# Modulation pieces of the later sections: loaded one step ahead of their sums, at other rates, and cut into two streams

## The chip, the cores and the metric

One core of a Trainium2 chip runs the whole program. The metric is device time in microseconds (us) of one execution. TensorE does the matmuls, VectorE (DVE) and ScalarE (ACT) the elementwise work, GpSimd (POOL) a little, SyncE (SP) issues nearly all loads. The time before is 2664.92 us, the median of 3 runs.

## The reference, cut to what matters

The program computes two transformer-like blocks on 256 tokens of width 2048. All that the change touches lies in the first block:

```python
mod = (c_act @ w_mod + b_mod)[:, None, :]          # w_mod: 2048 x 12288
sh1, sc1, gt1, sh2, sc2, gt2 = jnp.split(mod, 6, axis=-1)
h = rmsnorm(x, g_norm1) * (1 + sc1) + sh1
...                                                # projections w_in, GLA and mLSTM scans
x = x + gt1 * merge_groups(...)                    # ends in a product with w_out
h2 = rmsnorm(x, g_norm2) * (1 + sc2) + sh2
x = x + gt2 * conv_ffn(h2, ...)                    # w_up, a 3x3 convolution, w_down
```

The modulation vector `mod` is one vector of 2048 times a matrix of 2048 x 12288. Its six sections of 2048 columns are wanted at different times: sections 0 and 1 at once, section 2 (`gt1`) in the product with `w_out`, sections 3 and 4 (`sh2`, `sc2`) at the norm ahead of the FFN, section 5 (`gt2`) at the end of the FFN.

## The kernel before, in words

**Weights.** Every large product reads its weight in units of 512 KB (128 partitions x 1024 floats). `units` (from L189) yields them; `load_raw` (L168 to L173) takes one of the four `raw` buffers and has SP load it (L172). `split_w` then makes two halves of the number: ACT casts `raw` into `wh` (L187), DVE subtracts into `wl` (L188). There are four `wh` and four `wl` buffers. When L188 is done the `raw` buffer is free. TensorE multiplies from `wh` and `wl`: `a_form` has three matmuls per tile (L208 to L210), `b2_form` two (L237, L238).

**Modulation beside the weights.** Sections 2 to 5 are summed on DVE, not on TensorE. They make 16 blocks of 512 columns, and `mod_vec` treats a block in 8 steps. A step loads 512 KB of `w_mod` through the same `load_raw` and the same four `raw` buffers, and adds two rows of it, each scaled, into the tile `ev` (L514 for the first row of a block, L516 for the others). After the eighth step a small matmul (L523, L533 or L543) adds over the partitions and the result goes into `gtd` (section 2), `mod` (3 and 4) or `gtr` (5).

**What sets the order.** `Stream.tick` is called once per weight unit and takes `rate` steps of the stream. `MODS` holds the rates by part of the program: the second half of the inputs, keys (8 units of the mLSTM keys, and then 8 units of the GLA queries, for which no other rate is set), values (16 units), gates (40 units), output (32 units of `w_out`), FFN (240 units). A second stream, `side`, issues the scans' work in the same way. Up to the values SP follows the order of the code; from the gates on the framework's scheduler orders SP too. On the other engines it orders by readiness and by place in the code, with a bonus for L187 and L188. Each engine works through its own queue in order: an instruction that waits holds up what stands behind it.

**The end of `mix_out`.** After the last unit of `w_out` a loop (L1197) takes steps until twelve blocks are done, because the norm needs sections 3 and 4. Then `ple_fill(4)` gives TensorE four small products of the second block, `norm_T` makes `h2`, and the FFN begins. `x` is updated at L1189 and L1190, the row scale is made from L1214 and L258, the normalised rows are scaled at L1233 and L314. The second block has a place of the same shape, the product with `pool_w_out` (64 units, `out_product`) and what follows it, without any modulation beside it.

Of the kernel before, what the change touches and what calls it, by code (L numbers as in the profile page):

```python
# [6 lines left out]
F32 = mybir.dt.float32  # L7
# [3 lines left out]
ALU = mybir.AluOpType  # L11
# [3 lines left out]
P = 128  # L15
D = 2048
# [8 lines left out]
OUTG = ((0, 512), (512, 512), (1024, 512), (1536, 256), (1792, 256))  # L25
NG = len(OUTG)

MODS = {"inputs": 1.0, "keys": 1.0, "values": 1.25, "gates": 0.75, "output": 0.5, "ffn": 0.15}

SIDE = {"keys": 1.0, "queries": 1.0, "values": 1.4, "gates": 1.6, "attention": 1.3}  # L30
AHEAD = 1000
# [75 lines left out]
class Kern:  # L107
# [391 lines left out]
                nc.vector.tensor_tensor(out=dst, in0=dst, in1=wide(self.g1 if sec == 1 else self.g2), op=ALU.mult)  # L499
        yield 1  # L500

    def mod_vec(self, sec, blk):


        nc, a = self.nc, self.a
        c0 = sec * D + blk * 512
        ev = self.one([P, 512], "ev")
        for k0 in range(0, 16, 2):
            src = a["w_mod"][0, k0 * P:(k0 + 2) * P, c0:c0 + 512].rearrange("(k p) n -> p k n", p=P)
            _, rv = self.load_raw(src, 2, 512)  # L510
            for i in range(2):
                cc = self.cs[:, 2 * (k0 + i):2 * (k0 + i) + 1]
                if k0 + i == 0:
                    nc.vector.tensor_scalar(out=ev, in0=rv[:, i, :], scalar1=cc, scalar2=None, op0=ALU.mult)  # L514
                else:
                    nc.vector.scalar_tensor_tensor(out=ev, in0=rv[:, i, :], scalar=cc, in1=ev,  # L516
                                                   op0=ALU.mult, op1=ALU.add)
            if k0 < 14:
                yield 1
        if sec == 2:  # L520

            pt = self.ps()
            nc.tensor.matmul(pt[0:1], self.c("one"), ev, start=True, stop=True)  # L523
            b, g = self.t2(), self.t2()
            nc.sync.dma_start(b[0:1], a["b_mod"][0:1, c0:c0 + 512])
            nc.vector.tensor_tensor(out=g[0:1], in0=pt[0:1], in1=b[0:1], op=ALU.add)
            nc.scalar.dma_start(self.gtd[:, blk * 512:(blk + 1) * 512], g[0:1])
            yield 1
            return
        if sec == 5:  # L530

            pt = self.ps()
            nc.tensor.matmul(pt, self.c("one").broadcast_to([P, P]), ev, start=True, stop=True)  # L533
            if blk % 2 == 0:
                self.gtr.append(self.t4())
            b = self.t2()
            nc.sync.dma_start(b, a["b_mod"][0, c0:c0 + 512].partition_broadcast(P))
            nc.vector.tensor_tensor(out=self.gtr[-1][:, (blk % 2) * 512:(blk % 2 + 1) * 512], in0=pt, in1=b, op=ALU.add)
            yield 1
            return  # L540
        pv = self.ps()[:, :8].rearrange("p (k r) -> p k r", r=2)
        for q in range(4):
            nc.tensor.matmul(pv[:, q, :], ev[:, q * P:(q + 1) * P], self.c("one").broadcast_to([P, 2]),  # L543
                             start=True, stop=True)
        s = slice(blk * 4, blk * 4 + 4)
        wide = lambda v: v[:, s].unsqueeze(2).broadcast_to([P, 4, 2])
        dst = self.mod[sec][:, s, :]
        nc.vector.tensor_tensor(out=dst, in0=pv, in1=wide(self.bm[sec]), op=ALU.add)
        if sec == 4:
            nc.vector.tensor_tensor(out=dst, in0=dst, in1=wide(self.g2), op=ALU.mult)  # L550
        yield 1

    def mod_steps(self):
        self.gtr = []
        self.gtd = self.dram.tile([1, D], F32, name="gtd")
        for b in range(16):
            yield from self.mod_vec(2 + b // 4, b % 4)
            self.mods_done = b + 1


    def mix_in(self):
        nc, a = self.nc, self.a
# [25 lines left out]
        gates = self.t2((112, 2, T))  # L588
# [4 lines left out]
        blocks = [(k, k + 2) for k in range(0, 16, 2)]  # L593
        nb = len(blocks)

        def mod_block(b):
            lo, hi = blocks[b]
            return self.mod_pe(lo * P, (hi - lo) * P, (0, 1))

        def hidden(b, ti):  # L600
            kts = list(range(*blocks[b]))
            x, dst = (self.xt[2:4], hl) if ti == 0 else (self.xt[0:2], hc)
            self.xposed([(lambda kt, tt=tt: x[kt // 8][:, tt, kt % 8 * P:(kt % 8 + 1) * P]) for tt in range(2)], kts, dst,
                        scale=lambda kt: self.a1[:, kt, ti:ti + 1], shift=lambda kt: self.s1[:, kt, ti:ti + 1])
# [31 lines left out]
        def weights(b, i):  # L636
            if b < nb:
                ws[b, i] = list(self.units(w, 512 + 512 * i, 512, range(*blocks[b])))
# [10 lines left out]
        for b in range(nb):  # L649
            mods = mod_block(b + 1) if b + 1 < nb else iter(())  # L650

            if b == nb // 2:
                self.setup_later()
                self.mods_done = 0
                self.mods.set(self.mod_steps(), MODS["inputs"])
            weights(b + 1, 0)
            for i, _ in enumerate(pieces(b)):
                if i == 4:
                    weights(b + 1, 1)
                if i == 8:  # L660
                    weights(b + 1, 2)
                if i % 2 == 0:
                    next(mods, None)
                if i == 8 and b + 1 < nb:
                    hidden(b + 1, 0)
                if i == 10 and b + 1 < nb:
                    hidden(b + 1, 1)
# [25 lines left out]

        self.mods.rate = MODS["keys"]
        self.side.set(self.gla_context(gkc, gvc), SIDE["keys"])
# [10 lines left out]
        self.queries = True  # L706
        self.mods.rate = MODS["values"]
        self.side.rate = SIDE["values"]
# [200 lines left out]
    def mix_scan(self):  # L909
        nc, a = self.nc, self.a  # L910
        w = a["w_in"][0]
        self.mods.rate = MODS["gates"]
        gm = self.b8((P, 3, T))
# [248 lines left out]
    def mix_out(self):  # L1162
        nc, a = self.nc, self.a
        self.side.drain()
        self.mods.rate = MODS["output"]
        self.x = []
        for tt in range(2):
            t = self.b8()
            nc.sync.dma_start(t, a["x"][0, tt * P:(tt + 1) * P, :])
            self.x.append(t)  # L1170
        yT = self.act_pair(16)

        def src(tt):
            def f(kt):
                y = self.ygla if kt < 8 else self.yml
                return y[:, tt, (kt % 8) * P:(kt % 8 + 1) * P]
            return f
        self.xposed([src(0), src(1)], list(range(16)), yT)
        sums = self.sums(1)
        for g, (c0, n) in enumerate(OUTG):  # L1180
            s = slice(c0, c0 + n)
            gt = self.t2()[:, :n]
            nc.sync.dma_start(gt, self.gtd[0, s].partition_broadcast(P))
            accs = self.a_group(a["w_out"][0], c0, yT, range(16), n)
            with self.urgent(g == NG - 1):
                for tt in range(2):
                    t = self.t2()[:, :n]
                    x = self.x[tt][:, s]
                    nc.vector.tensor_tensor(out=t, in0=accs[tt], in1=gt, op=ALU.mult)  # L1189
                    nc.vector.tensor_tensor(out=x, in0=t, in1=x, op=ALU.add)  # L1190
                    self.square_sum(x, sums[:, 0, tt, g:g + 1])
        self.tap("x1", self.x[0])

        self.x1 = self.dram.tile([2, P, D], F32, name="x1")
        for tt in range(2):
            nc.sync.dma_start(self.x1[tt], self.x[tt])
        while self.mods_done < 12:  # L1197
            self.mods.step()
        self.ple_fill(4)
        with self.urgent():  # L1200
            rs = self.rstd(self.total(sums, 1)[:, 0], D, 2)
            self.h2 = self.norm_T(self.x, rs, scale=lambda kt: self.a2[:, kt, 0:1],
                                  shift=lambda kt: self.s2[:, kt, 0:1])
        self.mods.rate = MODS["ffn"]
        self.five = True

    def sums(self, kinds):
# [647 lines left out]
```

## Time and profile before

| what | value |
|---|---|
| median of 3 runs | 2664.92 us (2662.52 to 2669.27) |
| the profiled execution: its time / span of its instructions | 2672.57 us / 2670.4 us |
| share of the span: TensorE matmul, weight load, DVE, ACT | 97%, 82%, 69%, 48% |
| moved by the DMA engines | 558.89 MB, mean 209 GB/s |

The profiled execution is 7.65 us above the median, and 2.17 us of it lie outside its span. A busy TensorE in this profile is not one at its peak: matmuls are pipelined and their ends are modelled. Stages lie one after another: inputs to about 240 us, keys to 300, queries to 335, values to 455, gates to 614, the product with `w_out` to 717, the norm to 752, the FFN to 1505.

### The profile page before, as it was taken

How to read it: one execution, taken by the hardware profiler on the slowest of the kernel's cores; microseconds unless marked ns; L12 is line 12 of the kernel's file. 1: busy time of each engine (PE TensorE's matmuls, PEld its weight loads, DVE VectorE, ACT ScalarE, POOL GpSimd, SP SyncE). 2: the span in 40 equal slices, each digit the busy share in tenths (PEclk: the TensorE clock that was granted, in tenths of full speed). 3: DMA queues.
4: the chain of work that ended last, by engine and by line, in shares of the span. 5: the costliest groups of instructions: out<-in, count | busy, mean ns of one | idle time of the engine just before them, and what ended most of it. 6: DMA issues, size and time to landing. Idle time of an engine off the chain costs nothing.

```text
span 2670.4 us, 37499 instructions
## 1 busy us (share of the span) xinstructions
PE 2603.5 (97%) x14093; PEld 2190.4 (82%) x14093; DVE 1846.4 (69%) x3006; ACT 1281.8 (48%) x2008; POOL 26.5 (1%) x52
## 2 busy tenths in 40 slices
PE   5999999999899999999999999999999999999999
PEld 3666888877778888888888988888888889998888
DVE  4466678787778988857856867677755566666665
ACT  2223323344365555544534554555544455657553
POOL 1000000000000000000000000000000000000000
PEclk8999999999999999999999999999999999999999
DMA  9775466678876666666675666556665567645664
GB/s 333 246 239 173 143 211 199 226 224 265 274 260 220 210 220 206 226 218 205 204 243 179 215 190 189 190 189 189 197 232 189 185 208 215 166 143 173 201 217 159
DMA packets 345271, 558.89 MB, mean 209 GB/s; under 512 B 30692, under 2 KB 129178, under 8 KB 342402
## 3 DMA queue, kind: packets, MB, share of 16 engines
q1 hardware_dynamic: 339800, 548.54, 63.9%
q10 hardware_dynamic: 4746, 7.11, 0.7%
q8 instruction: 110, 1.80, 0.3%
q0 software_dynamic: 544, 0.86, 0.1%
q14 instruction: 71, 0.58, 0.1%
HBM read 541.75 MB, written 14.69 MB: 208 GB/s over the span
## 4 chain that ended last, share of the span: by engine, by line
PE 82%; DMA 8%; DVE 6%; ACT 2%; issue 2%; SPq 1%; POOL 0%; ACTq 0%; DVEq 0%
PE acc L237 20%; PE acc L210 10%; PE acc L208 10%; PE acc L209 10%; PE acc L238 10%; PE mod L237 5%; DMA raw<-in_w_in_dram 3%; PE mod L238 2%; PE mod L209 2%; PE mod L210 2%; PE mod L208 2%; DMA raw<-in_w_mod_dram 2%; DVE wl L188 2%; DMA raw<-in_w_out_dram 1%; DVE ev L516 1%
## 5 line engine op out<-in xcount | busy, mean ns | idle before, releaser
L188 DVE TENSOR_TENSOR wl<-raw,wh 128x1024 fp32r<-128x1024 f32 (+4 forms) x804 | 965.7, 1205 | 578.2 <-ACT wh L187 575.5
L187 ACT CAST wh<-raw 128x1024 fp32r<-128x1024 f32 (+4 forms) x804 | 829.6, 1036 | 1068.0 <-PE acc L210 345.7
L237 PE MATMUL acc<-b,wh 128*128 128x512 f32 x2336 | 821.1, 394 | 0.0
L238 PE MATMUL acc<-b,wl 128*128 128x256 f32 x2336 | 634.4, 281 | 1.1 <-DVE wl L188 1.0
L208 PE MATMUL acc<-wh,b 128*128 128x512 f32 (+3 forms) x1580 | 585.3, 373 | 10.0 <-ACT b L290 7.6
L209 PE MATMUL acc<-wl,b 128*128 128x512 f32 (+3 forms) x1580 | 586.6, 371 | 7.5 <-DVE wl L188 7.3
L210 PE MATMUL acc<-wh,b 128*128 128x512 f32 (+3 forms) x1580 | 576.2, 370 | 1.1 <-DVE b L291 0.6
L237 PEld LDWEIGHTS acc<-b,wh 128*128 128x128 f32 x2336 | 434.1, 188 | 88.9 <-issue 0.7
L238 PEld LDWEIGHTS acc<-b,wl 128*128 128x128 f32 x2336 | 438.9, 188 | 15.0 <-DVE wl L188 2.4
L208 PEld LDWEIGHTS acc<-wh,b 128*128 128x128 f32 x1580 | 298.8, 189 | 71.8 <-ACT b L290 9.4
L209 PEld LDWEIGHTS acc<-wl,b 128*128 128x128 f32 x1580 | 299.2, 189 | 62.1 <-DVE wl L188 12.6
L210 PEld LDWEIGHTS acc<-wh,b 128*128 128x128 f32 x1580 | 297.0, 189 | 55.6 <-DVE b L319 4.0
L516 DVE SCALAR_TENSOR_TENSOR ev<-raw,cs,ev 128x512 f32<-128x512 f32 x240 | 179.4, 747 | 59.1 <-DMA raw<-in_w_mod_dram 56.4
L237 PE MATMUL mod<-b,wh 128*128 128x512 f32 x576 | 215.5, 396 | 0.6 <-DVE t L249 0.6
L238 PE MATMUL mod<-b,wl 128*128 128x256 f32 x576 | 161.5, 280 | 0.7 <-DVE wl L188 0.7
L237 PEld LDWEIGHTS mod<-b,wh 128*128 128x128 f32 x576 | 108.4, 188 | 23.5 <-DVE t L249 1.1
L1367 DVE SCALAR_TENSOR_TENSOR t<-t,convw,t 128x189 f32<-128x189 f32 (+2 forms) x344 | 126.9, 423 | 0.0
L238 PEld LDWEIGHTS mod<-b,wl 128*128 128x128 f32 x576 | 108.3, 188 | 3.9 <-DVE wl L188 1.1
L208 PE MATMUL mod<-wh,b 128*128 128x512 f32 (+2 forms) x274 | 96.9, 354 | 0.0
L209 PE MATMUL mod<-wl,b 128*128 128x512 f32 (+2 forms) x274 | 96.7, 353 | 0.0
L210 PE MATMUL mod<-wh,b 128*128 128x512 f32 (+2 forms) x274 | 96.5, 352 | 0.0
L290 ACT CAST b<-t 128x256 fp32r<-128x256 f32 x123 | 47.2, 405 | 64.2 <-DVE t L314 44.1
(357 smaller groups left out, 2469.0 us busy)
## 6 DMA issues: line engine op xcount, KB each, us to landing
raw<-in_w_up_dram SPq DMA_DIRECT2D x160, 512.0 KB, 4.5
raw<-in_w_mod_dram SPq DMA_DIRECT2D x128, 512.0 KB, 4.5
raw<-in_pool_w_in_dram SPq DMA_DIRECT2D x128, 512.0 KB, 3.8
raw<-in_w_in_dram SPq DMA_DIRECT2D x96, 512.0 KB, 4.9
raw<-in_w_down_dram SPq DMA_DIRECT2D x83, 512.0 KB, 4.8
b<-in_w_mod_dram SPq DMA_DIRECT2D x64, 512.0 KB, 7.9
raw<-in_pool_w_out_dram SPq DMA_DIRECT2D x64, 512.0 KB, 4.0
raw<-in_ple_w_gate_dram SPq DMA_DIRECT2D x64, 512.0 KB, 3.9
```

What stands on the lines that cost most here:

```text
L187: nc.scalar.copy(wh[:, :n], raw[:, :n])
L188: nc.vector.tensor_tensor(out=wl[:, :n], in0=raw[:, :n], in1=wh[:, :n].bitcast(F32), op=ALU.subtract)
L208: mm(out, lh, rh, start=first, stop=False)
L209: mm(out, lh, rl, start=False, stop=False)
L210: mm(out, ll, rh, start=False, stop=last)
L237: mm(acc, wh[:, i, o], f.both(kt), start=kt == k_first, stop=False)
L238: mm(acc[:, :T], wl[:, i, o], f(kt)[0], start=False, stop=kt == k_last)
L290: nc.scalar.copy(h, src)
L516: nc.vector.scalar_tensor_tensor(out=ev, in0=rv[:, i, :], scalar=cc, in1=ev, op0=ALU.mult, op1=ALU.add)
L1367: nc.vector.scalar_tensor_tensor(out=ov[:, r0:r1, c0:c1], in0=uv[:, r0 + dy:r1 + dy, c0 + dx:c1 + dx], scalar=tap(ky, kx), in1=ov[:, r0:r1 ...
```

## The change

Four things. (1) `mod_steps` now takes a list of blocks and issues, in each step, first the load of the following step and then the sums of its own (a stream's first step issues two loads). (2) The rate beside keys and queries goes from 1.0 to 2.0, that beside the values from 1.25 to 1.0. (3) The first stream ends after 12 blocks (96 steps) and the last 4 blocks (32 steps) are a stream of their own that is set where the FFN begins, at the same 0.15. (4) `mod_vec` is now an ordinary function of one step.

```diff
-MODS = {"inputs": 1.0, "keys": 1.0, "values": 1.25, "gates": 0.75, "output": 0.5, "ffn": 0.15}
+MODS = {"inputs": 1.0, "keys": 2.0, "values": 1.0, "gates": 0.75, "output": 0.5, "ffn": 0.15}
...
+    def mod_steps(self, blocks):
+
+        todo = [(b, k0) for b in blocks for k0 in range(0, 16, 2)]
+
+        def load(b, k0):
+            c0 = (2 + b // 4) * D + b % 4 * 512
+            src = self.a["w_mod"][0, k0 * P:(k0 + 2) * P, c0:c0 + 512].rearrange("(k p) n -> p k n", p=P)
+            return self.load_raw(src, 2, 512)[1]
+        ahead = load(*todo[0])
+        for i, (b, k0) in enumerate(todo):
+            rv = ahead
+            if i + 1 < len(todo):
+                ahead = load(*todo[i + 1])
+            self.mod_vec(2 + b // 4, b % 4, k0, rv)
+            if k0 == 14:
+                self.mods_done = b + 1
+            yield 1
...
-    def mod_vec(self, sec, blk):
+    def mod_vec(self, sec, blk, k0, rv):
...
-        ev = self.one([P, 512], "ev")
-        for k0 in range(0, 16, 2):
-            src = a["w_mod"][0, k0 * P:(k0 + 2) * P, c0:c0 + 512].rearrange("(k p) n -> p k n", p=P)
-            _, rv = self.load_raw(src, 2, 512)
...
-    def mod_steps(self):
-        self.gtr = []
-        self.gtd = self.dram.tile([1, D], F32, name="gtd")
-        for b in range(16):
-            yield from self.mod_vec(2 + b // 4, b % 4)
-            self.mods_done = b + 1
...
-                self.mods.set(self.mod_steps(), MODS["inputs"])
+                self.mods.set(self.mod_steps(range(12)), MODS["inputs"])
...
-        self.mods.rate = MODS["ffn"]
+        self.mods.set(self.mod_steps(range(12, 16)), MODS["ffn"])
```

Steps by part of the program, from the rates and units: before 9 in the inputs, 16 in keys and queries, 20 in the values, 30 in the gates, 16 beside `w_out`, 5 in the loop L1197, 2 in `ple_fill`, 30 in the FFN. Now 9, 32, 16, 30, 9, none, none, 32.

The order of the instructions shows it at three places. The first is SP's queue where the mLSTM keys begin: `raw` from `w_in` is a unit of weights, `raw` from `w_mod` one step. Before:

```order
L172 DMA raw_1763<-in_w_mod_dram 128x2x512
L172 DMA raw_1777<-in_w_in_dram 128x2x512
L172 DMA raw_1807<-in_w_mod_dram 128x2x512
L172 DMA raw_1819<-in_w_in_dram 128x2x512
L172 DMA raw_1849<-in_w_mod_dram 128x2x512
L172 DMA raw_1861<-in_w_in_dram 128x2x512
```

Now:

```order
L172 DMA raw_1765<-in_w_mod_dram 128x2x512
L172 DMA raw_1769<-in_w_mod_dram 128x2x512
L172 DMA raw_1783<-in_w_in_dram 128x2x512
L172 DMA raw_1813<-in_w_mod_dram 128x2x512
L172 DMA raw_1817<-in_w_mod_dram 128x2x512
L172 DMA raw_1829<-in_w_in_dram 128x2x512
```

Two loads of modulation stand ahead of each unit in place of one, through both keys and queries.

The second is SP's queue in the middle of the product with `w_out`. Before:

```order
L172 DMA raw_5254<-in_w_out_dram 128x2x512
L172 DMA raw_5272<-in_w_mod_dram 128x2x512
L172 DMA raw_5276<-in_w_out_dram 128x2x512
L172 DMA raw_5306<-in_w_out_dram 128x4x256
L172 DMA raw_5336<-in_w_mod_dram 128x2x512
L172 DMA raw_5347<-in_w_out_dram 128x4x256
```

Now:

```order
L172 DMA raw_5140<-in_w_out_dram 128x2x512
L172 DMA raw_5158<-in_w_mod_dram 128x2x512
L172 DMA raw_5162<-in_w_out_dram 128x2x512
L172 DMA raw_5192<-in_w_out_dram 128x2x512
L172 DMA raw_5219<-in_w_out_dram 128x2x512
L172 DMA raw_5237<-in_w_out_dram 128x2x512
```

The load `raw_5158` is the last of the first stream; the 16 units of `w_out` behind it follow one another, where before every second unit had a load of `w_mod` ahead of it to the end.

The third is DVE's queue at the end of `mix_out` (`ev` is a sum of modulation, L1189 and L1190 update `x`, L1214 begins the row scale). Before:

```order
L516 SCALAR_TENSOR_TENSOR ev_5407<-raw_5605,cs,ev_5407 128x512 x2
L1189 TENSOR_TENSOR t_1009_5582<-acc_5452,t_992_5450 128x256
L516 SCALAR_TENSOR_TENSOR ev_5407<-raw_5609,cs,ev_5407 128x512
L1190 TENSOR_TENSOR b_855_4697<-t_1009_5582,b_855_4697 128x256
L516 SCALAR_TENSOR_TENSOR ev_5407<-raw_5609,cs,ev_5407 128x512
L1189 TENSOR_TENSOR t_1010_5586<-acc_5453,t_992_5450 128x256
L188 TENSOR_TENSOR wl_5644<-raw_5641,wh_5643 128x1024
L1190 TENSOR_TENSOR b_856_4699<-t_1010_5586,b_856_4699 128x256
```

Now (line numbers are 7 higher from here on):

```order
L1196 TENSOR_TENSOR t_1015_5609<-acc_5487,t_1000_5485 128x256
L1196 TENSOR_TENSOR t_1016_5613<-acc_5488,t_1000_5485 128x256
L1197 TENSOR_TENSOR b_870_4755<-t_1015_5609,b_870_4755 128x256
L1197 TENSOR_TENSOR b_871_4757<-t_1016_5613,b_871_4757 128x256
L188 TENSOR_TENSOR wl_5717<-raw_5714,wh_5716 128x1024
L323 TENSOR_TENSOR t_1017_5620<-ps_5625,t_1017_5620 128x256
L1221 TENSOR_REDUCE sm_5738<-sums_4835 128x2
```

No sum of modulation stands between the updates of `x` any more, nor among the norm that follows.

## Rows read from the trace of the kernel before

**Rows 1.** The page's first part: busy time, share of the span and instructions by engine.
```profile
span 2670.4 us, 37499 instructions
PE 2603.5 (97%) x14093; PEld 2190.4 (82%) x14093; DVE 1846.4 (69%) x3006; ACT 1281.8 (48%) x2008; POOL 26.5 (1%) x52
```
**Rows 2.** The chain that ended last, 240 to 300, 335 to 460, 460 to 614, 614 to 745.
```profile
by line: PE acc L209 24.0%; PE acc L208 23.8%; PE acc L210 23.8%; PE ps L816 8.6%; PE ps L786 6.7%; PE ps L803 5.7%; PE ps L805 2.9%; PE ps L775 1.6%; PE ps L523 1.6%; PE ps L684 1.5%; PE ps L630 0.2%
...
by line: DMA raw<-in_w_in_dram 36.9%; DVE wl L188 10.2%; DVE b L992 10.1%; ACT wh L187 8.6%; DVE b L998 7.0%; issue 6.9%; DVE ev L516 6.9%; DVE b L1008 5.9%; DMA mvd<-t 4.2%; DVE b L1015 1.8%; DVE ev L514 0.7%; DVE b L1059 0.5%; DVE t L526 
...
by line: DMA raw<-in_w_in_dram 21.7%; PE acc L208 12.3%; PE acc L209 11.9%; PE acc L210 11.8%; DVE ev L516 5.7%; PE ps L1123 5.5%; PE ps L879 4.8%; ACT wh L187 4.1%; PE ps L1120 3.7%; issue 3.5%; DMA mvd<-t 3.4%; PE ps L1095 2.8%; PE acc L1
...
by line: DMA raw<-in_w_mod_dram 31.7%; DMA raw<-in_w_out_dram 26.0%; DVE ev L516 8.9%; DVE wl L188 8.9%; issue 8.2%; ACT wh L187 6.8%; DMA raw<-in_ple_w_proj_dram 3.6%; DVE t L1189 1.3%; DVE b L1190 0.7%; ACT junk L1219 0.7%; DVE b L323 0.6
```
**Rows 3.** Busy time by stretch, us from the span's start (columns in the first row).
```profile
core 0: us, PE busy (x) PEld busy (x) DVE busy (x) ACT busy (x) POOL busy (x), PEclk, DMA share, GB/s
240.00:300.00 60.00, 60.00 (x237) 42.74 (x236) 36.99 (x55) 23.87 (x33) 0.00 (x0) 0.97 0.40 122
300.00:335.00 35.00, 35.00 (x227) 30.89 (x226) 22.54 (x29) 17.07 (x24) 0.00 (x0) 0.90 0.48 146
335.00:460.00 125.00, 120.34 (x617) 100.53 (x616) 103.35 (x128) 42.49 (x47) 2.29 (x5) 1.00 0.62 195
460.00:614.00 154.00, 150.16 (x738) 121.94 (x737) 115.68 (x228) 66.58 (x120) 6.24 (x7) 1.00 0.73 236
614.00:714.00 100.00, 93.98 (x470) 76.88 (x469) 71.77 (x94) 40.91 (x58) 0.00 (x0) 0.98 0.79 261
718.00:748.00 30.00, 20.66 (x95) 16.14 (x94) 21.20 (x41) 14.26 (x30) 0.70 (x1) 0.83 0.96 346
800.00:1300.00 500.00, 500.00 (x2728) 430.50 (x2727) 396.89 (x682) 256.70 (x376) 0.00 (x0) 1.00 0.67 215
1990.00:2090.00 100.00, 100.00 (x541) 85.85 (x540) 51.02 (x54) 43.75 (x58) 0.00 (x0) 1.00 0.57 189
2110.00:2130.00 20.00, 18.30 (x85) 13.44 (x84) 15.16 (x33) 12.54 (x25) 1.41 (x2) 1.00 0.67 208
```
**Rows 4.** ACT in order of time (start, us): first and last of 32 casts, `w_out`.
```profile
614.58 1.05 ACT L187 CAST wh<-raw 128x1024 fp32r<-128x1024 f32 x1 [0.29 <-DMA raw<-in_w_out_dram]
...
713.60 1.05 ACT L187 CAST wh<-raw 128x1024 fp32r<-128x1024 f32 x1 [2.56 <-DMA raw<-in_w_out_dram]
```
**Rows 5.** The same view: first and last of 37 casts, `pool_w_out`.
```profile
1986.22 1.05 ACT L187 CAST wh<-raw 128x1024 fp32r<-128x1024 f32 x1 [1.75 <-PE acc L210]
...
2086.78 1.05 ACT L187 CAST wh<-raw 128x1024 fp32r<-128x1024 f32 x1 [0.97 <-PE mod L210]
```
**Rows 6.** Who waited for whom (us in total, times, longest), 614 to 745.
```profile
ACT wh L187 <- DMA raw<-in_w_out_dram: 49.4, 25, 5.9
DVE ev L516 <- DMA raw<-in_w_mod_dram: 18.7, 11, 3.9
```
**Rows 7.** DVE in order of time at the norm ahead of the FFN.
```profile
741.37 0.75 DVE L516 SCALAR_TENSOR_TENSOR ev<-raw,cs,ev 128x512 f32<-128x512 f32 x1 [2.73 <-DMA raw<-in_w_mod_dram]
742.04 0.54 DVE L314 TENSOR_SCALAR t<-ps,mod,mod 128x256 f32<-128x256 f32 x1
```
**Rows 8.** The page's costliest groups: one sum of a row of modulation.
```profile
L516 DVE SCALAR_TENSOR_TENSOR ev<-raw,cs,ev 128x512 f32<-128x512 f32 x240 | 179.4, 747 | 59.1 <-DMA raw<-in_w_mod_dram 56.4
```
**Rows 9.** SP in order of time (start, length with its waits), 403 to 437.
```profile
412.25 0.37 SPq L172 DMA_DIRECT2D raw<-in_w_in_dram  x1
418.26 15.77 SPq L172 DMA_DIRECT2D raw<-in_w_mod_dram  x2
435.23 1.94 SPq L172 DMA_DIRECT2D raw<-in_w_in_dram  x2
```
**Rows 10.** What SP's queue waited for, 335 to 460.
```profile
SPq L172 <- DVE ev L516: 51.3, 22, 14.9
SPq L172 <- DVE wl L188: 37.7, 18, 4.4
```

More of the change, by code (lines that the diff above doesn't have):

```diff
@@ L500, in mod_pe @@
         yield 1
-    def mod_vec(self, sec, blk):
+    def mod_steps(self, blocks):
[14 more added lines that the diff above has]
+    def mod_vec(self, sec, blk, k0, rv):
         nc, a = self.nc, self.a
         c0 = sec * D + blk * 512
-        ev = self.one([P, 512], "ev")
-        for k0 in range(0, 16, 2):
-            src = a["w_mod"][0, k0 * P:(k0 + 2) * P, c0:c0 + 512].rearrange("(k p) n -> p k n", p=P)
-            _, rv = self.load_raw(src, 2, 512)
[L511 to L519, printed above, removed]
+        if k0 == 0:
+            self.ev = self.one([P, 512], "ev")
+        ev = self.ev
+        for i in range(2):
+            cc = self.cs[:, 2 * (k0 + i):2 * (k0 + i) + 1]
+            if k0 + i == 0:
+                nc.vector.tensor_scalar(out=ev, in0=rv[:, i, :], scalar1=cc, scalar2=None, op0=ALU.mult)
+            else:
+                nc.vector.scalar_tensor_tensor(out=ev, in0=rv[:, i, :], scalar=cc, in1=ev, op0=ALU.mult, op1=ALU.add)
+        if k0 < 14:
+            return
         if sec == 2:
@@ L527, in mod_vec @@
             nc.scalar.dma_start(self.gtd[:, blk * 512:(blk + 1) * 512], g[0:1])
-            yield 1
             return
@@ L538, in mod_vec @@
             nc.vector.tensor_tensor(out=self.gtr[-1][:, (blk % 2) * 512:(blk % 2 + 1) * 512], in0=pt, in1=b, op=ALU.add)
-            yield 1
             return
@@ L550, in mod_vec @@
             nc.vector.tensor_tensor(out=dst, in0=dst, in1=wide(self.g2), op=ALU.mult)
-        yield 1
-    def mod_steps(self):
-        self.gtr = []
-        self.gtd = self.dram.tile([1, D], F32, name="gtd")
-        for b in range(16):
-            yield from self.mod_vec(2 + b // 4, b % 4)
-            self.mods_done = b + 1
     def mix_in(self):
@@ L653, in mix_in @@
                 self.setup_later()
-                self.mods_done = 0
-                self.mods.set(self.mod_steps(), MODS["inputs"])
+                self.mods_done, self.gtr = 0, []
+                self.gtd = self.dram.tile([1, D], F32, name="gtd")
+                self.mods.set(self.mod_steps(range(12)), MODS["inputs"])
             weights(b + 1, 0)
```

## The prediction

> **What bounds the kernel now.** I read the page's first part, then the chain of waits cut into stages, then the busy times of the same stages, and last the waits of single instructions. TensorE looks full, 97% of the span [rows 1], so at first there seems to be nothing to win. The chain says otherwise, and by stage. From 240 to 300 (mLSTM keys) it runs through matmuls alone [rows 2]: TensorE is the limit, and DVE is busy for 37.0 of 60 us, with 122 GB/s moved [rows 3]. From 335 to 460 (values) no large share of it is a matmul: 36.9% is the load of `w_in`, the rest casts, splits and scan work on DVE [rows 2]. That is a loop through the four `raw` buffers: a split ends, SP issues the next load, it lands, ACT casts, DVE splits. DVE has 103.4 us of work in these 125 [rows 3]. From 614 to 745 (`w_out` and the norm) the largest share, 31.7%, is the load of `w_mod`, ahead of the 26.0% of `w_out` itself [rows 2]: the modulation is on the path here. In the FFN TensorE is busy all 500 of 500 us [rows 3]. So a modulation step costs nothing beside the keys and in the FFN, and most at `w_out`; the change moves steps between just these places.
>
> **The change, part by part.** A step is 512 KB of load, one `raw` buffer and two sums of 0.747 us on DVE [rows 8], so 1.5 us of DVE. From the rates the steps go: keys and queries 16 to 32, values 20 to 16, gates 30 to 30, `w_out` with the loop and `ple_fill` 16 + 5 + 2 = 23 to 9, FFN 30 to 32.
>
> *The product with `w_out`.* Its 32 units are cast from 614.58 to 713.60 [rows 4]: 99.0 us over 31 intervals, 3.19 us a unit. The product with `pool_w_out` has units of the same form without modulation: 37 casts from 1986.22 to 2086.78 [rows 5], 100.6 us over 36, 2.79 us a unit, and there the cast waits for TensorE, at `w_out` for the load. A freed unit is worth 0.40 us. In the new order the last 16 units have no modulation among them: 16 x 0.40 = 6.4 us. The first 16 keep one load to two units, but the sums no longer stand right behind their load; DVE waited 18.7 us for such loads from 614 to 745 [rows 6]. That is worth between nothing and another 6.4 us; I take 1.6, since the loads themselves stay. Together **-8**, ends -13 and -5.
>
> A second reading of the same gain. TensorE is idle for only 6.0 of the 100 us from 614 to 714 [rows 3], which would allow no more than 6. The Trainium skill, Perfetto Trace Analysis, section Identifying the Most-Contended Engine, says that matmul busy time is a poor measure of the distance from the limit, since matmuls are pipelined, and that the busy time of the weight loads is a better one. By weight loads the stretch has 76.9 us against 85.9 in the 100 us of `pool_w_out` [rows 3], so it could be done in 76.9 / 85.9 x 100 = 89.6 us and up to 10.4 us are to be had. By the idle time this term would be capped at 6 and my sum would be 2 us smaller; the paces of units, which need neither, stand with the larger figure.
>
> *The end of `mix_out`.* Seven steps go from here (loop and `ple_fill`): 14 sums, 10.5 us of DVE, and 3.7 MB. Now TensorE has 20.7 busy of 30 us from 718 to 748, at a granted clock of 0.83, while 346 GB/s are moved; the same passage behind `pool_w_out`, 2110 to 2130, has 18.3 of 20 at a clock of 1.00 [rows 3]. Idle time is 9.3 us here and 1.7 there, so up to 7.6 us, and a few more from the clock, can come back. At the least it is the 2.7 us for which DVE stands at a sum whose load is late, with a scaling of the norm queued right behind it [rows 7]. The passage here must also store `x` and has twice the `ple` units, so not all of it returns: **-8**, ends -12 and -3.
>
> *Keys and queries.* 16 more steps: 8.4 MB, 24 us of DVE. Half fall in the keys, where matmuls are the chain: 37.0 + 12 = 49 us of DVE in 60, and room for 4.2 MB at 122 GB/s. Cover enough: 0. What hides it is TensorE's own work; if that cover is gone, up to 12 us. The queries are light units: DVE goes from 22.5 to 34.5 us in 35 [rows 3], all of it. If DVE packs no better than in the values (103.4 of 125, 83%), the stage needs 34.5 / 0.83 = 42 us, 7 more. By loads it has 24 in place of 16 (12.6 MB): at the 346 GB/s of 718 to 748 that takes 36 us, 1 more; at its own old pace of one load in 35 / 16 = 2.2 us it takes 53, 18 more. Units that were split ahead during the keys take some of it up. I take **+5**, nearest to the DVE figure, ends 0 and +18.
>
> *Values.* 4 steps fewer, 6 us of DVE where DVE is short. SP's queue waited 51.3 us in this stage for sums to free a `raw` buffer [rows 10], at the worst between 418 and 434, when sums stood behind scan work on DVE and no weight was issued from 412.3 to 435.2 [rows 9]. Fewer sums thin this; but each sum now stands one step later behind its own load. I take **-4**: 6 us of DVE less a third for sums that close later. Ends -20 (the 15.8 us stall goes too) and +6.
>
> *Gates.* 30 steps as before, each load one step earlier: **-1**, ends -6 and +6 by the two sides of the same effect. *FFN.* Two steps more, 3 us of DVE beside a TensorE that is never idle: 0, and below 3 if the cover fails. The second half of the inputs has one more load in flight under TensorE: 0.
>
> **Sum:** -8 - 8 + 5 - 4 - 1 = -16 us. Against the profiled execution that is 2672.6 - 16 = 2656.6. That execution is 7.7 above the median of the runs, so for the median I forecast 2664.9 - 16 = **2649**. A measurement of this kernel can tell about 0.3%, 8 us, from no change.
>
> **Rivals.** *The ring's stall goes as well (faster still).* If the long wait of SP in the values disappears, that term is -20 in place of -4: 2633. For it: the stall is one bunch of sums. Against it: DVE stays full. Chance 0.12.
>
> *The queries give it back (no change).* The 24 loads go at the queries' old pace, +18 in place of +5, and the first half of `w_out` and the values bring little: -6.4 - 8 + 18 - 4 = 0, say 2662. For it: DVE would have 34.5 of 35 us. Against it: the lead from the keys. Chance 0.18.
>
> *Load-ahead takes a buffer away (slower).* A step's buffer is now held from its load over one whole step. If the sums really close that late, one of four `raw` buffers is lost to the weights wherever the ring is what ends last. The chain has 36.9% of 125 us in weight loads in the values, 46 us; losing one buffer of four makes three do the work, a third more, +15; some 34 us (26.0% of 131) at `w_out`, half of whose units still have steps, +6; and in the gates 21.7% of 154 us [rows 2], 33 us, a third +11. -16 + 32 = +16: 2681. It decides from the point where most sums close after the fourth load behind their own. For it: SP already waits most for sums [rows 10]. Against it: readiness orders DVE, not the place in the code. Counted in the two orders, a step's last sum stands on average 1.1 splits behind the weights loaded ahead of it in the values, and 1.3 now; in the gates 0.5, and 0.7 now: a fraction of a unit. Chance 0.12.
>
> That the change doesn't do what it says is excluded by the order: the loads stand earlier and the loop at the end has nothing left.
>
> **How the numbers follow.** The forecast has what is left, 0.58. Its own range is 2638 to 2657, the terms' ends taken not all on one side. The range reaches up over most of the no-change case and down to the faster one: 2633 to 2667; beyond it lie the slower case and a little on the low side. Faster by over 0.3% (under 2657): 0.58 + 0.12 = 0.70. Within 0.3%: 0.18. Slower: 0.12.
>
> **What would show it.** Right: no load of `w_mod` between the last unit of `w_out` and the first of `w_up`; the last 16 casts of `w_out` at 2.9 us or less; DVE's waits for `w_mod` in that stretch from 18.7 to under 6 us; under 5 us of TensorE idle in the passage to the FFN; queries longer by 3 to 8 us; SP's waits for sums in the values below 45 us. Wrong: a passage as long as before, for then it hung on the row scale and the stores, not on the modulation; queries longer by 15 us or more; or the FFN, which is to keep its length within 3 us, growing.

## The result, and the profile after

The changed kernel takes 2686.97 us, the median of 4 runs (2686.11 to 2692.45), beside 2665.64 for the kernel before on the same chip: a ratio of 1.0084, 95% interval 1.0065 to 1.0103. It is slower by 21 us, where 16 us less were forecast, and lies above the forecast's range, which ended at 2667. The profiled execution took 2686.50 us. The one of before lies 7 us above its median, so the two traces differ by only 14 of the 21 us.

The page's first part, columns as in [rows 1]:

```profile
span 2684.6 us, 37498 instructions
PE 2608.5 (97%) x14093; PEld 2195.9 (82%) x14093; DVE 1849.7 (69%) x3006; ACT 1280.2 (48%) x2007; POOL 26.0 (1%) x52
```

The work is the same; TensorE's busy time grew by 5.0 us, and the rest is time without work. Busy times by stretch, of the kernel after, show where [rows 3]:

```profile
core 0: us, PE busy (x) PEld busy (x) DVE busy (x) ACT busy (x) POOL busy (x), PEclk, DMA share, GB/s
240.00:300.00 60.00, 58.28 (x232) 40.54 (x231) 37.82 (x61) 19.17 (x26) 0.00 (x0) 1.00 0.44 141
300.00:335.00 35.00, 27.66 (x159) 22.24 (x157) 26.90 (x35) 15.54 (x20) 0.00 (x0) 0.92 0.61 197
320.00:340.00 20.00, 12.06 (x66) 10.09 (x64) 17.35 (x24) 7.40 (x7) 0.00 (x0) 0.74 0.53 164
340.00:360.00 20.00, 14.43 (x81) 14.03 (x82) 13.26 (x18) 4.64 (x7) 0.00 (x0) 0.74 0.79 267
718.00:748.00 30.00, 29.03 (x222) 27.80 (x221) 18.75 (x27) 14.06 (x25) 0.70 (x1) 1.00 0.66 224
```

Before, TensorE was never idle from 240 to 335; now it stands for 13.5 of the 40 us from 320 to 360. DVE did no more from 240 to 300 than before (37.8 us against 37.0), though twice as many sums were to be done there: something held the sums up. The last row is the other side: the passage that had 20.7 us of work in 30 has 29.0.

To count it by stage I use the casts of the weight units as milestones (the times of those views of ACT that [rows 4] come from), and TensorE's idle time between the same milestones (gaps of over 0.15 us between its matmul records, added up in the stage in which they begin):

| stage (units between the casts) | forecast | casts, after less before | TensorE idle before | after |
|---|---|---|---|---|
| inputs, to unit 24 | 0 | +2.0 | 30.6 | 32.2 |
| keys and queries, 24 to 40 | +5 | +32.9 | 1.4 | 19.8 |
| values, 40 to 56 | -4 | -22.3 | 1.9 | 0.4 |
| gates, 56 to 96 | -1 | +13.5 | 6.5 | 4.9 |
| `w_out`, 96 to 127 (idle: to 128) | -8 | -8.3 | 10.3 | 4.3 |
| passage, 127 to 160 (idle: from 128) | -8 | -5.2 | 6.6 | 5.2 |
| all later | 0 | +2.0 | 4.2 | 3.9 |
| sum | -16 | +14.6 | 61.6 | 70.6 |

Casts run some units ahead of TensorE. In keys and queries they lost that lead (+32.9) and in the values they won much of it back (-22.3); TensorE itself stands idle for 18.4 us more in keys and queries.

**What held the sums up.** SP's queue in order of time where the keys' weights are loaded, of the kernel after (a length takes in the waits between the parts of a group):

```profile
223.24 0.37 SPq L172 DMA_DIRECT2D raw<-in_w_in_dram  x1
225.03 0.37 SPq L172 DMA_DIRECT2D raw<-in_w_mod_dram  x1
247.60 0.25 SPq L541 DMA_DIRECT2D t<-in_b_mod_dram  x1
247.94 0.37 SPq L172 DMA_DIRECT2D raw<-in_w_mod_dram  x1
248.40 0.42 SPq L172 DMA_DIRECT2D raw<-in_w_in_dram  x1
248.91 13.45 SPq L172 DMA_DIRECT2D raw<-in_w_mod_dram  x2
266.04 0.37 SPq L172 DMA_DIRECT2D raw<-in_w_in_dram  x1
```

From 225.4 to 247.6 SP issues nothing. It stands at L541, the bias row that closes a block of modulation; then it stands again, until 262. In 43 us one unit of weights is issued (248.40). Who kept it waiting, from 205 to 305, is in the view of waits, and below it what TensorE waited for from 200 to 460:

```profile
SPq L541 <- PE ps L691: 22.1, 1, 22.1
SPq L172 <- DVE ev L533: 17.6, 12, 3.4
SPq L172 <- DVE t L841: 9.4, 1, 9.4
```

```profile
PE acc L208 <- ACT wh L187: 13.3, 7, 4.3
PE acc L208 <- ACT b L290: 4.4, 1, 4.4
```

The row goes into a `t2` buffer, which came free with transposes at the end of the inputs (L691), late in TensorE's queue. The second stand has to do with the block itself. DVE and TensorE in order of time, of the kernel after:

```profile
225.03 1.54 DVE L533 SCALAR_TENSOR_TENSOR ev<-raw,cs,ev 128x512 f32<-128x512 f32 x2
...
260.76 1.21 DVE L188 TENSOR_TENSOR wl<-raw,wh 128x1024 fp32r<-128x1024 f32 x1
...
263.37 0.68 DVE L542 TENSOR_TENSOR t<-ps,t 1x512 f32<-1x512 f32 x1
263.98 0.47 DVE L531 TENSOR_SCALAR ev<-raw,cs 128x512 f32<-128x512 f32 x1
```

```profile
262.31 1.02 PE L539 MATMUL ps<-ev,cst 128*1 128x512 f32 x2
...
296.25 1.02 PE L539 MATMUL ps<-ev,cst 128*1 128x512 f32 x2
...
319.84 1.02 PE L539 MATMUL ps<-ev,cst 128*1 128x512 f32 x2
```

The block is summed at 226.6. The matmul that closes it, L539, runs at 262.31, since it stands in TensorE's queue behind units that SP and DVE had run ahead of. There is one `ev`, so the next block's first sum (L531) comes at 263.98, 37 us later, and the loads of its steps (225.03, 247.94, 248.91) hold three of the four `raw` buffers until then. Only the fourth goes on. SP's stand to 262, 9.4 us of which the view puts down to L841 on DVE, ends as the split of the one unit in that buffer ends (L188, 260.76 + 1.21); the next unit, at 266.04, is issued once the new block's first step is summed. A closing matmul comes at every eighth step, again at 296 and at 320; there DVE is without a sum for 9.6 and 3.8 us.

The kernel before has the same stop, and I had not read it. Its DVE and TensorE at the same place:

```profile
241.82 0.74 DVE L516 SCALAR_TENSOR_TENSOR ev<-raw,cs,ev 128x512 f32<-128x512 f32 x1
...
286.12 0.47 DVE L514 TENSOR_SCALAR ev<-raw,cs 128x512 f32<-128x512 f32 x1
```

```profile
284.46 1.02 PE L523 MATMUL ps<-ev,cst 128*1 128x512 f32 x2
```

There no sum is done from 242.56 to 286.12, and TensorE is not idle at all. At one step to a unit SP came to the boundary only at 236.7 (it stood 4.9 us at the row), with weights issued up to unit 29 and not 26, and one load of `w_mod`, not two, went into the ring for each unit that followed.

**`w_out`.** Here the forecast held. The chain of waits of the kernel after, from 640 to 748 (its `w_out` and norm [rows 2]), and ACT's first and last of 32 casts there [rows 4], with the two ahead of the last:

```profile
by line: PE acc L209 23.7%; PE acc L208 23.3%; PE acc L210 23.1%; DMA raw<-in_w_out_dram 19.2%; DVE wl L188 5.7%; ACT wh L187 5.6%; PE ps L557 0.7%; issue 0.6%; ACT t L322 0.3%; ACTq L187 0.1%; DVE b L323 0.0%
```

```profile
640.62 1.05 ACT L187 CAST wh<-raw 128x1024 fp32r<-128x1024 f32 x1 [1.13 <-DMA raw<-in_w_out_dram]
...
725.63 1.05 ACT L187 CAST wh<-raw 128x1024 fp32r<-128x1024 f32 x1 [1.79 <-PE acc L210]
728.49 1.05 ACT L187 CAST wh<-raw 128x1024 fp32r<-128x1024 f32 x1 [1.81 <-PE acc L210]
731.33 1.05 ACT L187 CAST wh<-raw 128x1024 fp32r<-128x1024 f32 x1 [1.78 <-PE acc L210]
```

Loads of `w_mod` led the chain with 31.7%; they are gone from it, and matmuls make 70%. The casts take 90.7 us against 99.0, the last ones 2.85 us apart, held by TensorE and not by a load. DVE's wait for `w_mod`, 18.7 us [rows 6], is now this:

```profile
DVE ev L533 <- DMA raw<-in_w_mod_dram: 0.3, 1, 0.3
```

### The profile page after: what moved, and what is told of

Its sections match the earlier page's. It is cut to its first block, busy times and chain, and to the rows that moved or that the text cites. A ratio compares the mean times of both kernels' runs of the same rounds, so it can differ in the third digit from the quotient of the medians.

```text
span 2684.6 us, 37498 instructions
## 1 busy us (share of the span) xinstructions
PE 2608.5 (97%) x14093; PEld 2195.9 (82%) x14093; DVE 1849.7 (69%) x3006; ACT 1280.2 (48%) x2007; POOL 26.0 (1%) x52
## 4 chain that ended last, share of the span: by engine, by line
PE 88%; DMA 5%; DVE 3%; ACT 2%; SPq 1%; issue 1%; POOL 0%; ACTq 0%; DVEq 0%
PE acc L237 20%; PE acc L208 12%; PE acc L210 12%; PE acc L209 12%; PE acc L238 10%; PE mod L237 5%; PE mod L238 2%; DMA raw<-in_w_in_dram 2%; PE mod L208 2%; PE mod L210 2%; PE mod L209 2%; DVE wl L188 1%; PE ps L208 1%; ACT wh L187 1%; PE ps L209 1%; PE ps L210 1%
## 5 line engine op out<-in xcount | busy, mean ns | idle before, releaser
L188 DVE TENSOR_TENSOR wl<-raw,wh 128x1024 fp32r<-128x1024 f32 (+4 forms) x804 | 966.0, 1205 | 596.0 <-ACT wh L187 588.1
L208 PE MATMUL acc<-wh,b 128*128 128x512 f32 (+3 forms) x1580 | 580.8, 374 | 20.5 <-ACT b L290 11.7
L208 PEld LDWEIGHTS acc<-wh,b 128*128 128x128 f32 x1580 | 298.5, 190 | 81.0 <-ACT b L290 13.5
L208 PE MATMUL acc<-b,wh 128*128 128x256 f32 x232 | 70.8, 308 | 11.5 <-ACT wh L187 11.5
```

The source lines that it names most:

```text
L188: nc.vector.tensor_tensor(out=wl[:, :n], in0=raw[:, :n], in1=wh[:, :n].bitcast(F32), op=ALU.subtract)
L208: mm(out, lh, rh, start=first, stop=False)
```

## The experiments

Theories for the loss, by the letters that some expectations use: A, the bias row's wait in SP's queue alone; B, the doubled rate beside keys and queries as such (more loads and sums than ring and DVE bear); C, loading ahead as such (a step's buffer held longer); and, formed after the first runs, D, the block boundary: one `ev`, closed by a matmul far back in TensorE's queue, with the bias row as its second half. Ratios are to the kernel before, timed on the same chip beside it; its medians there were 2666 to 2670 us.

**The bias row from another queue** (`e1_row_pool`, on the changed kernel):

```diff
-            nc.sync.dma_start(b[0:1], a["b_mod"][0:1, c0:c0 + 512])
+            nc.gpsimd.dma_start(b[0:1], a["b_mod"][0:1, c0:c0 + 512])
```

> The changed kernel, with the small load of the bias row (L541) issued by GpSimd in place of SyncE. Theory A (SyncE's queue stands at this row until the inputs' transposes free its buffer, and the keys' weights stand behind it): the 22 us wait is gone from SyncE, cast 28 comes about 20 us earlier than in the changed kernel, and the time falls from 2687 to about 2667. Theory B (two loads per weight unit overload the four raw buffers and DVE in keys and queries, whatever the row does): cast 40 stays 25 to 35 us later than before, time 2682 to 2687. Theory C (load-ahead holds a buffer): as B.

Measured: 2689.75 us, ratio 1.0072 (1.0055 to 1.0089): nothing gained. What SP waited for from 205 to 305, and SP's queue there:

```profile
SPq L172 <- DVE ev L533: 47.4, 14, 21.4
```

```profile
235.23 9.43 SPq L172 DMA_DIRECT2D raw<-in_w_mod_dram  x2
266.09 0.37 SPq L172 DMA_DIRECT2D raw<-in_w_in_dram  x1
```

The row no longer stops SP, but SP stops all the same, 21.4 us at a load that wants a `raw` buffer back from a sum of the next block. A alone falls; two waits stand one behind the other, and taking the first away shows the second.

**The change in its parts** (`e2_old_rates`: rates 1.0 and 1.25 again, load-ahead and two streams stay. `e5_no_ahead`: the new rates and two streams, loads issued as before. `e4_cut_only`: two streams alone).

```diff
# e2_old_rates, on the changed kernel
-MODS = {"inputs": 1.0, "keys": 2.0, "values": 1.0, ...
+MODS = {"inputs": 1.0, "keys": 1.0, "values": 1.25, ...
# e5_no_ahead, on the kernel before
-MODS = {"inputs": 1.0, "keys": 1.0, "values": 1.25, ...
+MODS = {"inputs": 1.0, "keys": 2.0, "values": 1.0, ...
# e4_cut_only and e5_no_ahead, on the kernel before
-    def mod_steps(self):
-        self.gtr = []
-        self.gtd = self.dram.tile([1, D], F32, name="gtd")
-        for b in range(16):
+    def mod_steps(self, blocks):
+        for b in blocks:
...
-                self.mods.set(self.mod_steps(), MODS["inputs"])
+                self.mods.set(self.mod_steps(range(12)), MODS["inputs"])
...
-        self.mods.rate = MODS["ffn"]
+        self.mods.set(self.mod_steps(range(12, 16)), MODS["ffn"])
```

> The changed kernel with the rates of before (keys 1.0, values 1.25): load-ahead and the two streams alone. A and B: the keys cost nothing, five steps remain for the loop at the end, time 2656 to 2668. C: each step's buffer is lost to the weights here too, time 2675 or more.

> The kernel before with the new rates and the two streams, without load-ahead. A: the bias row stands ahead of the same weights, SyncE waits 15 to 25 us there, time 2675 to 2690. B: keys and queries are overloaded as well, time 2675 to 2690, but without a long single wait of SyncE. C: without load-ahead nothing is held, time 2645 to 2660.

> The kernel before with the two streams alone (the steps for section 5 begin at the FFN; rates and order of load and sum as before). All theories: two steps leave the passage to the FFN, five stay in the loop; 0 to 4 us faster than before, 2661 to 2666.

Measured: `e2_old_rates` 2679.37, ratio 1.0040 (1.0025 to 1.0055); `e5_no_ahead` 2675.15, 1.0026 (1.0014 to 1.0038); `e4_cut_only` 2671.41, 1.0004 (0.9992 to 1.0016). The two streams cost nothing. Load-ahead costs 0.36% at the old rates (1.0040 against 1.0004) and 0.58% at the new (1.0084 against 1.0026); the rates cost 0.22% without it and 0.44% with it. Each seems to make the other dearer, as if they met in one place, but that difference, 0.22%, is no larger than the intervals: it is a guess for the next runs. `e2_old_rates` came out in the range that theory C gave it. With the new rates alone SP stops at the same row, whose `t2` buffer now comes free by DVE (issued at 242.77), and TensorE starves (waits of SP from 205 to 335 and of TensorE from 200 to 340, of `e5_no_ahead`):

```profile
SPq L525 <- DVE t L769: 17.2, 1, 17.2
```

```profile
PE acc L208 <- ACT wh L187: 9.9, 2, 7.7
```

**Both halves of the boundary removed** (`e9_two_ev`: a second `ev`, room taken from `t1`; `e9b_two_ev_row`: the same and the row from GpSimd; `e10_before_two_ev_row`: the same three edits on the kernel before, as a control; `e12_no_ahead_two_ev_row`: on `e5_no_ahead`; a later tile with the same tag, `rrow`, gets the second buffer too).

```diff
-        return self.pool.tile(list(shape), dt, tag="t1", bufs=6, name=self.nm("t1"))
+        return self.pool.tile(list(shape), dt, tag="t1", bufs=4, name=self.nm("t1"))
...
-            self.ev = self.one([P, 512], "ev")
+            self.ev = self.pool.tile([P, 512], F32, tag="ev", bufs=2, name=self.nm("ev"))
...
-            nc.sync.dma_start(b[0:1], a["b_mod"][0:1, c0:c0 + 512])
+            nc.gpsimd.dma_start(b[0:1], a["b_mod"][0:1, c0:c0 + 512])
...
-        self.rrow = self.one([P, 512], "ev")[:, :T]
+        self.rrow = self.pool.tile([P, 512], F32, tag="ev", bufs=2, name=self.nm("ev"))[:, :T]
```

> The changed kernel with two ev tiles in place of one (t1 goes from six buffers to four to make room). Theory D (between two blocks of modulation the next sum must wait until TensorE's queue comes to the closing matmul, since there is one ev; the loads already made hold raw buffers for that time and SyncE stands): the 39 us on DVE without a sum go, but SyncE still stands at the bias row, so the cast of unit 28 comes back by less than 10 us; time 2675 to 2690. Theory C (a load held for one step takes a buffer of the ring, boundary or not): nothing changes, 2687.

> Two ev tiles, and the bias row issued by GpSimd: both waits at a boundary are gone from SyncE. D: the cast of unit 28 comes 15 to 25 us earlier than in the changed kernel, and what remains at the end is 10 us or more: 2665 to 2678. B (two loads a unit overload ring and DVE): cast 40 stays 25 us or more behind before, time 2680 or more. C: 2680 or more.

> The kernel before with two ev tiles, the bias row issued by GpSimd, and t1 with four buffers: a control for the smaller t1, and D's boundary taken away where the rates are the old ones. D: the boundaries of before cost little, 0 to 6 us faster, 2660 to 2668; slower than 2675 would mean that t1 with four buffers costs time by itself.

> New rates and two streams without load-ahead, with two ev tiles and the bias row issued by GpSimd. D: the boundary was what made the new rates slow here too, 2655 to 2665, and load-ahead is then worth within 5 us of nothing beside the kernel with load-ahead and the same two edits. C: 10 us or more faster than that kernel. B: 2670 or more.

Measured: `e9_two_ev` 2678.03, ratio 1.0033 (1.0017 to 1.0048); `e9b_two_ev_row` 2671.65, 1.0012 (1.0000 to 1.0024); `e12_no_ahead_two_ev_row` 2671.52, 1.0019 (1.0003 to 1.0035); `e10_before_two_ev_row` 2679.58, 1.0048 (1.0033 to 1.0063). From the changed kernel to `e9b_two_ev_row` the ratio falls by 0.72%, 19 us. That is near to what TensorE had lost in keys and queries, but it is made of other parts: in the two traces its idle time falls by 18.2 us there and by 9.2 in all, since gates and `w_out` take 9.0 back, and its busy time falls by 12.0 us, in an execution of `e9b_two_ev_row` that is itself 6.5 us under its median. SP, then DVE at the boundary in `e9b_two_ev_row`, and what TensorE waits for from 200 to 460:

```profile
223.37 0.37 SPq L172 DMA_DIRECT2D raw<-in_w_in_dram  x1
224.95 5.12 SPq L172 DMA_DIRECT2D raw<-in_w_mod_dram  x2
232.22 0.37 SPq L172 DMA_DIRECT2D raw<-in_w_in_dram  x1
232.89 3.36 SPq L172 DMA_DIRECT2D raw<-in_w_mod_dram  x2
236.54 0.43 SPq L172 DMA_DIRECT2D raw<-in_w_in_dram  x1
```

```profile
228.14 1.53 DVE L533 SCALAR_TENSOR_TENSOR ev<-raw,cs,ev 128x512 f32<-128x512 f32 x2
230.58 0.48 DVE L531 TENSOR_SCALAR ev<-raw,cs 128x512 f32<-128x512 f32 x1
```

```profile
PE acc L208 <- ACT b L290: 1.6, 1, 1.6
PE ps L636 <- DVE b L620: 1.2, 1, 1.2
```

The next block's first sum follows at 230.58, not at 263.98; the wait for a cast (13.3 us) is gone from TensorE's list, and its idle time in keys and queries is 1.6 us. All rates and loads are those of the changed kernel, so B falls as its cause. And with the boundary open, loading ahead (`e9b_two_ev_row`) and not (`e12_no_ahead_two_ev_row`) give times within each other's intervals: C falls as well for these rates. That load-ahead cost what it did by putting one more load into the ring ahead of a closed block fits this, but no run shows it by itself.

Theory D's forecast for `e12_no_ahead_two_ev_row`, 2655 to 2665 us, was missed. Beside `e5_no_ahead` TensorE's idle time in keys and queries falls from 16.2 to 0.6 us, and yet the ratio (1.0019) can't be told from 1.0026: in values, gates and `w_out` TensorE stands idle for 12.6 us more, 8.0 of them in a wait that is told of below. Without load-ahead the closed boundary starves TensorE in keys and queries as well, but opening it won no time.

Between `e9_two_ev` and `e9b_two_ev_row` lie 0.21%, some 6 us (the intervals of the two ratios overlap a little), for one row of 2 KB from another queue, though alone it had won nothing. What SP waits for at the row in `e9_two_ev`, from 205 to 305:

```profile
SPq L541 <- PE ps L691: 18.9, 1, 18.9
```

The Trainium skill, Trainium Kernel Development and Optimization, section Key Constraints, says that issuing DMAs from several engines only saves the sequencer's issue time. This pair of runs shows more: the row's issue takes 0.25 us in the trace, and what else the edit takes away is an 18.9 us wait in front of the loads in SP's queue.

The control was a surprise: the same edits make the old kernel slower by 0.48%. Beside its boundary TensorE was never idle, so nothing was to be won. Its casts reach the gates 19.6 us sooner, and by the first cast of `w_out` it is 2.3 us ahead; then the product with `w_out` loses it, 16.6 us idle against 10.3, with a new wait at its start:

```profile
PE acc L208 <- ACT b L322: 7.3, 1, 7.3
```

**Where the room comes from, and the old rates** (`e13_two_ev_row_t2`: as `e9b_two_ev_row`, with six `t1` and five `t2`; `e14_old_rates_two_ev_row_t2`: that with the old rates; `e15_before_t1_4`: the kernel before with four `t1`, nothing else).

```diff
# e13_two_ev_row_t2, on e9b_two_ev_row
-... tag="t1", bufs=4 ...
+... tag="t1", bufs=6 ...
-... tag="t2", bufs=6 ...
+... tag="t2", bufs=5 ...
```

> The changed kernel with two ev buffers and the bias row issued by GpSimd, as in the run before, but the room for the second ev is taken from t2 (5 buffers for 6) and t1 keeps its 6. In the run with 4 t1 buffers TensorE stood 6.7 us at the start of the product with w_out (L208 for the cast L322), and its w_out units took 98.7 us where the changed kernel's take 90.7. Theory (both waits at a block's boundary are what the change lost by, t1 alone kept the rest hidden): w_out near 91 us, no wait over 2 us at its start, time 2671.7 - 7 = 2664 (2659 to 2668), a ratio to before of 0.998 or less. Rival (the room costs wherever it is taken from: five t2 delay the transposes of the inputs, or w_out is as long for another reason): 2671 or more.

> As the run beside it, with the old rates beside keys (1.0) and values (1.25): loads one step ahead and two streams stay. Theory (with the boundary's waits gone the rates themselves cost nothing, and what they are worth is the lighter w_out): some 5 us slower than the run beside it, 2669 (2664 to 2675), the loss in the passage from w_out to the FFN. Rival (the doubled rate costs by its work on DVE and its loads in the queries, whatever the boundary does): 3 us or more faster than the run beside it, 2660.

> The kernel before with 4 t1 buffers in place of 6, and nothing else: a control for the room that two ev tiles took. Theory: 7 us slower than before, 2675 (ratio 1.002 to 1.004), with the wait of L208 for L322 at the start of w_out. Rival (the control with two ev tiles was slower by the row on GpSimd or by the second ev itself): within 3 us of before.

Measured: 2673.43, ratio 1.0006 (0.9993 to 1.0018); 2680.22, 1.0043 (1.0027 to 1.0059); 2667.14, 0.9995 (0.9984 to 1.0007). Four `t1` cost nothing, so my account of the control by its room was wrong. `e13_two_ev_row_t2` was to win 7 us over `e9b_two_ev_row` and did not (the intervals overlap). And `e14_old_rates_two_ev_row_t2` repeats the control: with two `ev` the old rates are slower by 0.37% than the new, and lose it in `w_out` (18.0 us idle against 7.2), where their steps beside the product are more.

The wait at the start of `w_out` comes with the second `ev` itself. The six versions that have two stand there for 6.0 to 8.0 us at one place, with the row on either queue, four or six `t1`, old or new rates; in the eight with one `ev` no gap there is over 1.6 us. TensorE's wait in `e9b_two_ev_row`, and its DVE at that time:

```profile
PE acc L208 <- ACT b L322: 6.7, 1, 6.7
```

```profile
621.39 1.54 DVE L533 SCALAR_TENSOR_TENSOR ev<-raw,cs,ev 128x512 f32<-128x512 f32 x2 [1.70 <-DMA raw<-in_w_mod_dram]
...
626.61 0.75 DVE L533 SCALAR_TENSOR_TENSOR ev<-raw,cs,ev 128x512 f32<-128x512 f32 x1 [0.81 <-DMA raw<-in_w_mod_dram]
627.28 0.68 DVE L914 TENSOR_TENSOR b<-b,t 128x512 f32<-128x512 f32 x1
```

L914 makes the gated output, which L322 then casts for the product. It stands in DVE's queue behind sums that wait for their loads. So an open boundary has a price of its own: the order of DVE changes with it. Why the scheduler orders so was not tried.

**Steps taken from `w_out` and the loop, put beside the gates** (`e16_gates_rate`, on `e4_cut_only`):

```diff
-... "values": 1.25, "gates": 0.75, ...
+... "values": 1.25, "gates": 1.0, ...
```

> The kernel before with the two streams (none beyond twelve blocks until the FFN) and the rate beside the gates at 1.0 in place of 0.75: the ten steps that the passage to the FFN and the end of w_out lose stand beside the gates, where DVE is busy for 115 of 154 us, and not beside the keys. No load is issued ahead. Theory (the forecast's gain at w_out and behind it is real, some 6 to 11 us of TensorE's idle time, and what the changed kernel lost was the keys' block boundary alone): TensorE's idle time from the first w_out cast to the FFN falls from 15 to 9 us or less, the gates grow by no more than 4 us of idle time, time 2664 (2660 to 2669), a ratio of 0.9985 or a little less. Rival (time gained ahead of the FFN is taken up by the next wait: the gated output at the start of w_out and the norm's own products): the gates or the start of w_out lose what the passage wins, 2668 or more, ratio 1.000 to 1.004.

Measured: 2685.46 us, ratio 1.0063 (1.0043 to 1.0084). From the first cast of `w_out` to unit 160 TensorE's idle time is 6.4 us against 16.9 before, as the theory had it; but in the gates it is 20.5 us against 6.5, not up to 4 more. Busy times of its gates, and its chain of waits there:

```profile
460.00:637.00 177.00, 158.63 (x745) 123.85 (x743) 132.65 (x255) 66.96 (x126) 6.04 (x7) 0.98 0.73 239
```

```profile
by line: DMA raw<-in_w_in_dram 37.9%; DVE ev L516 9.2%; ACT wh L187 9.0%; DVE wl L188 8.6%; issue 8.1%; PE ps L1122 3.3%; DMA raw<-in_w_out_dram 3.0%; PE acc L208 2.7%; DMA raw<-in_w_mod_dram 2.5%; PE acc L209 2.5%; PE ps L1119 2.4%; PE acc
```

DVE has 44 us to spare in these 177, and still ten steps cost 14: the loop through the ring (load, cast, sum, split) leads the chain, as it led that of the values before [rows 2]. DVE's share said nothing about it.

No version beat the kernel before by more than its interval.

## Why the prediction was wrong

**Keys and queries, the step that failed.** "Cover enough: 0" counted DVE's time and bytes, and both do suffice. In `e9b_two_ev_row`, with the same rates, DVE has 48.8 us of work in the 60, as counted, 204 GB/s are moved, and TensorE is never idle (columns as in [rows 3]):

```profile
240.00:300.00 60.00, 60.00 (x240) 41.93 (x239) 48.81 (x73) 22.60 (x31) 1.45 (x3) 1.00 0.65 204
```

What it didn't count is the order of the queues. Steps are not independent: each eighth closes a block through TensorE's queue, and the next cannot be summed before. The working took 16 more steps as 16 times one step; they were two more block boundaries, and at two steps to a unit a block is only four units long. Forecast +5 with an upper end of +18; measured +32.9 by casts, 18.4 us in TensorE's idle time, and more in its clock. That the stand is the boundary's is shown: the three versions with the new rates and one `ev` are idle for 16 to 20 us there (19.8, 19.3, 16.2), `e9_two_ev` for 4.3, the three with two `ev` and the row elsewhere for 2.2 or less. In time it is shown for the kernel with load-ahead, where 1.0084 falls to 1.0033 with the second `ev` and to 1.0012 with the row moved too; without load-ahead opening the boundary won nothing that the runs can tell.

**The slower rival** named load-ahead and 2681 us. The time is near (2681 and 2687), but in part by chance. It put the loss into values, gates and `w_out`, where TensorE's idle time fell; with the boundary open load-ahead costs nothing that these runs can tell. Right in it was that loads made early hold buffers: they did so in the keys, ahead of a closed block. I had weighed it by splits between a load and its sum, where no closed block stands between them. At the old rates load-ahead costs 0.36% with the boundary closed, and with it open the time is the same (1.0040 and 1.0043), a new wait of 7.9 us in it: what load-ahead costs there stays open.

**`w_out`, -8:** right in the number, 8.3 us by casts, 5.9 in TensorE's idle time (the prediction's second reading, by idle time, allowed 6). **Passage, -8:** right in kind; -5.2, within its ends. The idle time from 718 to 748 went from 9.3 to 1.0 us, but some came back in the FFN's first units: 2.6 us of idle time more between units 136 and 160, part of it at the norm's transposes (L305). **FFN, 0:** right, +2.0 for all behind unit 160, within the 3 us given. **Values -4, gates -1:** together -8.9 by casts, which is in part the lead won back; by idle time -1.5 and -1.6. SP's waits for sums in the values fell from 51.3 to 43.8 us in the same stretch, as forecast; the time was not there.

**The gain at `w_out` does not come free either.** With the boundary open the terms that held (-8.3 and -5.2) should have left some 13 us of gain, and there is none. `e9b_two_ev_row` has 7.7 us idle in `w_out` (the changed kernel 4.3, before 10.3) and 10.5 in the gates (before 6.5), and its 32 casts take 98.8 us, as long as before (99.0). Of the idle time in `w_out` 6.7 us are the wait for L322 that came with the second `ev`. So the freed steps may have won their 8 us there and the wait taken most of it; or part of the gain that the changed kernel shows at `w_out` is its own loss given back. These runs do not part the two. Of the 17 to 18 us that the old rates with two `ev` stand idle in `w_out`, 7.3 and 7.9 are the same wait; the rest is left open.

## What to carry to other kernels

Before more background work is laid beside a stage, look for the tile that its pieces share and for what closes it: a closing step in the queue of an engine that lags by several units stops the whole background at each block, and every load behind it holds a buffer. The trace of before shows this even where it costs nothing (here 44 us without a sum, beside a full TensorE): read gaps of the background work itself, not only the busy time of the engines and the idle time of the bound one. A second tile opens the block, but it also lets the background run ahead of other work in the same queue (here 6 to 8 us at the start of `w_out`): read the next stage too. Two waits can stand one behind the other in an in-order queue; removing one alone then shows nothing, so test them together as well.

## What the runs showed beyond that

The starved stretch also cost clock: the granted clock was 0.74 from 320 to 360, a mean of the levels 1.2 and 2.4 GHz, while TensorE was busy 12.1 and 14.4 of 20 us; before, with TensorE busy throughout, it was at 1.00 from 320 to 360. With the boundary open (`e9b_two_ev_row`) it is at 1.00 there too. In the whole trace TensorE's busy time is 5.0 us longer for the same number of instructions, beside 9.0 us of idle time: a third of the traces' difference. How much of the 5.0 comes from this stretch is not shown.
